# Both products of a gated MLP from seven half products instead of eight, activations stored to DRAM between them

## The chip, the cores and the metric

The kernel runs on one core of one Trainium2 chip. The metric is the device time of one execution in microseconds; the lower, the better. One execution was profiled too: its times are those of the rows below. TensorE is called PE in the rows, VectorE DVE, ScalarE ACT, GpSimd POOL; SP issues most of the DMAs.

## The reference, cut to what matters

A decoder block on 1024 positions of width 1024 in float32: two mixers (sparse attention and retention), merged, an output projection with residual, then an MLP and a final norm. The change lies in the MLP and in what surrounds it:

```python
x = x + (gate_a * y_a + gate_b * y_b) @ w_mix_out[layer]
h = rms_norm(x, norm_ffn_w[layer])
u = causal_dwconv(h @ w_ffn_up[layer], ffn_conv_w[layer], ffn_conv_b[layer])   # 1024 x 5632, width 3
u_gate, u_val = jnp.split(u, 2, axis=-1)
x = x + (jax.nn.silu(u_gate) * u_val) @ w_ffn_down[layer]                      # 2816 x 1024
return rms_norm(x, norm_final_w)
```

## The kernel before

Each float32 product is made in three passes (`mm3`): both operands are split into a high and a low part of the type float32r, and high by high, high by low and low by high are summed in PSUM. A split is one copy on ACT (`wh`, L209, or `ah`, L175) and one subtraction (`wl` on POOL, L215; `al` on DVE, L176). One matmul has 128 rows of contraction, 128 columns of the stationary operand and 512 moving columns.

The output projection (`mo`, from L1044) makes 8 position tiles of 128 in two channel halves. In the second half each tile gets its residual, its RMSNorm and, by `transposed_split`, its place in `h2T`, the transposed and split input of the MLP. Tiles 6 and 7 come out together at the end; their transposes are put between the first up products.

The MLP goes over 11 groups of 256 channels. `up(j)` makes four column tiles (two of the gate, two of the value) over 8 contraction tiles and both halves of the positions, 192 matmuls; `conv` takes each from PSUM: ACT makes the tap of the same position with the bias (L1068), DVE adds the other two (L1069, L1070). Silu, the product with the value (L1095) and the split follow, and the activations stay in SBUF. `down(j-1)` then makes 96 matmuls on the group before, and DVE adds each result to the residual `xr` (L1113). So up and down products take turns, and the weights of a group are loaded by SP and split on ACT and POOL during the group before. The final norm of each tile (`final`, L1116) follows its last down product. A list of instructions is fixed for each engine when the kernel is built; an engine takes them one after the other, each behind the semaphores it waits for.

Of the kernel before, what the change touches and what calls it, by code (L numbers as in the profile page):

```python
# [18 lines left out]
P = 128  # L19
# [144 lines left out]
def hybrid_block(ctx: ExitStack, tc: tile.TileContext, a, c, out):  # L164
# [16 lines left out]
    class Weights:  # L181
        """Rows [k0*128, (k0+nk)*128) by up to 512 columns, split into the two parts of float32r."""
# [46 lines left out]
    def rstd_steps(pool, v):  # L229
        """v ** -0.5, the table's root improved by one step; yields after the root"""  # L230
# [21 lines left out]
    def mean_square(pool, parts, junk):  # L252
        """mean over D of the squares of the parts, plus eps; one part at a time"""
# [15 lines left out]
    def transposed_split(psum, src, hi, lo, t, nk=KT, tag="tp"):  # L269
        """src [128 s, nk*128] -> hi, lo [128, nk, s-tile t]"""  # L270
# [19 lines left out]
    # ---- first norm, transposed and split  # L290
# [7 lines left out]
    big = ctx.enter_context(tc.tile_pool(name="big", bufs=8, side="right"))  # L298
# [77 lines left out]
    def k_store(b, t, ps):  # L376
        """ps [p, (g d)] -> roped, transposed and split keys"""
# [45 lines left out]
    # ---- compressed keys and values  # L423
# [97 lines left out]
    # ---- the three attention branches  # L521
# [5 lines left out]
    def mm3t(ps, w, n0, act, nk, halves=(0, 1)):  # L527
        """ps[n, s] = w columns n0..n0+128 against act(part, kt)"""
# [36 lines left out]
    def scores(box, wait, t, g, bs, rank, last_pe):  # L565
        """Branches bs, the first two in one pass over their keys.
# [625 lines left out]
```

## Time and profile before

| | us |
|---|---|
| median of 3 runs | 1845.14 |
| lowest, highest run | 1844.7, 1846.16 |
| span of the profiled execution, first to last instruction | 1842.4 |
| PE busy in it | 1810.4 (98%) |
| DVE, ACT, POOL busy | 964.9, 694.8, 212.0 |
| up products, start of the first to start of the last matmul | 1105.0 to 1785.2 |
| down products | 1197.3 to 1828.7 |

The profiled execution was not timed apart from its span, so its own time is the span, 1842.4 us; the median of the runs is 2.7 us above that, for what lies ahead of the first and behind the last instruction. A share of busy time is a mean over the span; what bounds a stage is read from that stage.

### The profile page before, as it was taken

The numbers are of one execution on the slowest core, as the hardware profiler recorded it, in microseconds if no ns is written. First come the engines' busy times: TensorE is split into PE (matmuls) and PEld (weight loads), VectorE is DVE, ScalarE is ACT, GpSimd is POOL, SyncE is SP. The second block draws the span as 40 slices with busy tenths as digits, with TensorE's granted clock in tenths as the row PEclk, the third lists the DMA queues.
The fourth block names the chain that finished last, engine by engine and source line by source line (L and its number), as shares of the span: only waits on it lengthen the run. The fifth ranks groups of instructions, "written<-read, shape, count | busy, mean of one in ns | idle before, by whom it ended". The sixth has DMA issues, their size and how long they took to land.

```text
span 1842.4 us, 22342 instructions
## 1 busy us (share of the span) xinstructions
PE 1810.4 (98%) x8727; PEld 1500.7 (81%) x8727; DVE 964.9 (52%) x2062; ACT 694.8 (38%) x1283; POOL 212.0 (12%) x107
## 2 busy tenths in 40 slices
PE   8999999999999999999999999999999999999997
PEld 6987888878788888888888887888888888888885
DVE  7446878777774554564444254344333433424446
ACT  6335676666652352245522133312212211221224
POOL 0000020100000000000000012323113212311204
PEclk9999999999999999999999999999999999999998
DMA  6221020110202111101422411212112102201102
GB/s 223 68 67 52 24 64 24 41 47 24 67 31 81 46 47 46 47 24 46 162 91 79 151 35 30 78 54 69 35 35 69 51 18 69 69 23 46 58 0 103
DMA packets 70230, 110.18 MB, mean 60 GB/s; under 512 B 5532, under 2 KB 37868, under 8 KB 70124
## 3 DMA queue, kind: packets, MB, share of 16 engines
q1 hardware_dynamic: 68828, 104.03, 17.8%
q10 hardware_dynamic: 1296, 4.72, 0.6%
q8 instruction: 68, 1.11, 0.3%
q14 instruction: 38, 0.31, 0.1%
HBM read 96.15 MB, written 12.58 MB: 59 GB/s over the span
## 4 chain that ended last, share of the span: by engine, by line
PE 68%; issue 2%; DVE 2%; ACT 1%; DMA 1%; POOL 0%; SPq 0%; DVEq 0%; ACTq 0%; POOLq 0%
PE up L283 25%; PE mm L283 21%; PE dn L283 12%; PE fill L771 2%; PE mo L283 2%; PE po L825 1%; PE pv L717 1%; PE pt L705 1%; PE sc L609 1%; DMA wr<-in_w_ffn_up 1%; PE pst L825 1%; DVE rs_r L246 1%; PE tp L275 0%; PE pss L870 0%; ACT h L1130 0%
## 5 line engine op out<-in xcount | busy, mean ns | idle before, releaser
L283 PE MATMUL up<-h2T,wh 128*128 128x512 f32 x1408 | 434.0, 389 | 0.2 <-ACT h2T L175 0.2
L215 POOL TENSOR_TENSOR wl<-wr,wh 128x1024 fp32r<-128x1024 f32 x78 | 188.2, 2420 | 1490.4 <-ACT wh L209 1425.8
L283 PEld LDWEIGHTS up<-h2T,wh 128*128 128x128 f32 x1408 | 264.1, 188 | 55.6 <-ACT h2T L175 0.5
L283 PE MATMUL up<-h2T,wl 128*128 128x512 f32 x704 | 274.0, 389 | 0.0
L209 ACT ACTIVATE wh<-wr 128x1024 fp32r<-128x1024 f32 (+1 forms) x138 | 143.2, 1046 | 265.0 <-DMA wr<-in_w_ffn_up 90.2
L1069 DVE SCALAR_TENSOR_TENSOR y<-up,cw,y 128x1023 f32<-128x1023 f32 x44 | 56.4, 1283 | 343.2 <-ACT y L1068 343.2
L283 PE MATMUL mm<-wh,hh 128*128 128x512 f32 (+1 forms) x576 | 224.2, 389 | 0.3 <-ACT hh L175 0.3
L283 PE MATMUL mm<-wh,hl 128*128 128x512 f32 (+1 forms) x576 | 220.0, 382 | 0.0
L283 PE MATMUL mm<-wl,hh 128*128 128x512 f32 (+1 forms) x576 | 219.8, 382 | 0.0
L1068 ACT ACTIVATE y<-up,cw 128x1024 f32<-128x1024 f32 x44 | 53.0, 1204 | 282.7 <-PE up L283 282.5
L283 PEld LDWEIGHTS up<-h2T,wl 128*128 128x128 f32 x704 | 132.2, 188 | 27.5
L1113 DVE TENSOR_TENSOR xr<-dn,xr 128x512 f32<-128x512 f32 x176 | 118.3, 687 | 62.0 <-PE dn L283 62.0
L283 PE MATMUL dn<-wh,ah 128*128 128x512 f32 x352 | 137.1, 390 | 0.1
L283 PE MATMUL dn<-wh,al 128*128 128x512 f32 x352 | 137.0, 389 | 0.0
L283 PE MATMUL dn<-wl,ah 128*128 128x512 f32 x352 | 137.0, 389 | 0.0
L283 PEld LDWEIGHTS mm<-wh,hl 128*128 128x128 f32 x576 | 108.8, 189 | 20.5 <-DVE hl L176 0.3
L283 PEld LDWEIGHTS mm<-wh,hh 128*128 128x128 f32 x576 | 108.9, 189 | 19.9 <-ACT hh L175 0.7
L283 PEld LDWEIGHTS mm<-wl,hh 128*128 128x128 f32 x576 | 108.9, 189 | 19.5 <-DVE wl L215 0.5
L712 DVE TENSOR_TENSOR pl<-pt,ph 128x512 fp32r<-128x512 f32 (+1 forms) x148 | 100.6, 687 | 41.8 <-ACT ph L709 41.2
L709 ACT ACTIVATE ph<-pt 128x512 fp32r<-128x512 f32 (+1 forms) x148 | 87.6, 594 | 82.8 <-PE pt L705 74.5
L771 PE MATMUL fill<-hh,wh 128*128 128x512 f32 x256 | 104.5, 408 | 3.1 <-ACT sg L783 2.1
L627 ACT ACTIVATE big<-big,st 128x640 f32<-128x640 f32 (+7 forms) x128 | 93.4, 730 | 28.1 <-DVE st L623 27.5
(228 smaller groups left out, 3041.6 us busy)
## 6 DMA issues: line engine op xcount, KB each, us to landing
wr<-in_w_ffn_up SPq DMA_DIRECT2D x88, 256.0 KB, 3.2
wr<-in_w_in SPq DMA_DIRECT2D x40, 512.0 KB, 3.7
wr<-in_w_ffn_down SPq DMA_DIRECT2D x22, 512.0 KB, 3.6
gate<-sg SPq DMA_DIRECT2D x32, 256.0 KB, 2.0
wr<-in_w_in SPq DMA_DIRECT2D x16, 256.0 KB, 3.1
wr<-in_w_ret_branch SPq DMA_DIRECT2D x8, 512.0 KB, 4.2
ma<-gate SPq DMA_DIRECT2D x8, 512.0 KB, 6.6
gb<-gate SPq DMA_DIRECT2D x8, 512.0 KB, 7.5
```

The source lines that it names most:

```text
L209: nc.scalar.activation(hi[:, :, :self.n], self.raw[len(self.hi)], AF.Copy)
L215: self.engine.tensor_tensor(lo[:, :, :self.n], self.raw[j], f32(self.hi[j][:, :, :self.n]), OP.subtract)
L246: nc.vector.scalar_tensor_tensor(r, t, -3.0, half, op0=OP.add, op1=OP.mult)
L283: nc.tensor.matmul(ps, stat(sp, kt), mov(mp, kt), start=(first and n == 0), stop=(last and n == 3 * nk - 1))
L627: nc.scalar.activation(probs[b][h], probs[b][h], AF.Exp, scale=-1.0, bias=stat["nm", b][:, h:h + 1], accum_out=stat["w", b][:, h:h + 1])
L709: nc.scalar.activation(bx["h"][:rows], bx["pt"][:rows], AF.Copy)
L712: nc.vector.tensor_tensor(bx["l"][:rows], bx["pt"][:rows], f32(bx["h"][:rows]), OP.subtract)
L771: nc.tensor.matmul(fx["ps"], w.at(sp, kt, i * P, P), hT[mp][:, kt, half * 512:half * 512 + 512], start=(n == 0), stop=(n == 3 * KT - 1))
L825: nc.tensor.matmul(ps[:, h, :], stat[sp][:, h, :], mov[mp][:, h, :], start=(first and n == 0), stop=(last and n == 2))
L1068: nc.scalar.activation(y, ps, AF.Identity, scale=cw[:, 2, f:f + 1], bias=cw[:, 3, f:f + 1])
L1069: nc.vector.scalar_tensor_tensor(y[:, 1:], ps[:, :S - 1], cw[:, 1, f:f + 1], y[:, 1:], op0=OP.mult, op1=OP.add)
L1113: nc.vector.tensor_add(xo, ps, xo)
```

## The change

Everything up to the `mo` products is the same. Behind them both products of the MLP are made by Strassen's scheme in its form of Winograd: positions, contraction and columns are each halved, and seven products of halves of sums are made in place of eight products of halves. The sums are made in float32 ahead of the split.

For up, the columns of the weight are paired by the gate and the value tile of one `f` (22 of them), laid out by the host so that one `f` is one row of 8 KB for each partition (`_up_layout`). The input is cut into quarters by position half and contraction half; three quarters are split as they are (`bh`/`bl` 11, 21, 22), and four sums t1 to t4 are split by `sums(t)`, into memory that is free only when the `mo` products are done. An `f` is seven products of 12 matmuls. What they share is added up on DVE: u2, u3, then cv and cg, the two columns that the convolution reads, now from SBUF. The activations are stored to DRAM (`act_d`), and x1, the residual, too (`x1_d`).

Down starts when up has ended. Its seven products (p1, p2, p5, p6, p3, p7, p4 in that order) run over 11 contraction tiles in six steps of two (`STEPS`) and four position tiles `q`, 132 matmuls each. A step has its operands loaded anew, the weights into a ring of two raw tiles (`wraw`), the activations into tiles that are partly kept (`held`); sums go to POOL (activations) and DVE (weights), and `parts2` splits both. The four position tiles of the first half are normed behind p3, the others behind p4.

```diff
     for ch in range(2):
...
+                if waiting:
+                    piece(*waiting.pop())
+                waiting.append((t, h))
         gw = nx
+    bigs.close()
...
+    for k in ("t1", "t2", "t3", "t4"):
+        bh[k], bl[k] = (tpp.tile([P, 4, 512], F32R, name=f"{part}{k}") for part in ("bh", "bl"))
+
+    def sums(t):
+        at = slice((t - 4) * P, (t - 3) * P)
+        (t1, t4), (t3, t2) = low[t - 4], low[t]
+        for k, x, e in (("t2", t2, nc.gpsimd), ("t3", t3, nc.vector), ("t1", t1, nc.vector), ("t4", t4, nc.gpsimd)):
+            split(bh[k][:, :, at], bl[k][:, :, at], x, e)
+
+    for t in range(4, NT - 1):
+        sums(t)
+    piece(*waiting.pop())
+    sums(NT - 1)
...
+    def parts2(src, engine, cnt=2):
...
+        nc.scalar.activation(hi[:, :cnt], src[:, :cnt], AF.Copy)
+        engine.tensor_tensor(lo[:, :cnt], src[:, :cnt], f32(hi[:, :cnt]), OP.subtract)
+        return hi, lo
...
+    def up(f, w, begun=None):
+        x, p1 = begun or start_up(w)
+        y = bank()
+        prod(y, w["s2"], "t2")
+        u2 = c2()
+        nc.vector.tensor_add(u2, y, p1)
+        q = bank()
+        prod(q, w["s3"], "t3")
+        u3 = c2()
+        nc.vector.tensor_add(u3, q, u2)
+        z = bank()
+        prod(z, w["s1"], "t1")
+        cg, cv = c4(), c4()
+        nc.vector.tensor_add(cv[:, 1], z, u3)
+        if not begun:
+            prod(x, w["a12"], "21", False, True)
+        nc.scalar.activation(cg[:, 0], x, AF.Copy)
+        prod(q, w["a22"], "t4", False, True)
+        nc.vector.tensor_add(cv[:, 0], q, u2)
+        prod(z, w["s4"], "22", False, True)
+        nc.vector.tensor_add(cg[:, 1], z, u2)
+        yg = conv(cg.rearrange("p a b -> p (a b)"), f)
...
+        for n in range(2):
+            nc.sync.dma_start(act_d[f][n], yg[:, n * 512:n * 512 + 512])
...
+    def p5_ops(i, j, n):
+        s, t = store(S2, i), store(T2, i)
+        x, y = held(0, 1, j, n), held(1, 1, j, n)
+        nc.gpsimd.tensor_tensor(s[:, :n], x[:, :n], y[:, :n], OP.add)
+        y, x = raw_w(0, 0, j, n), raw_w(0, 1, j, n)
+        return s, diff(x, y, n, nc.vector, t)
...
+    def p7_ops(i, j, n):
+        s = diff(held(0, 0, j, n), held(0, 1, j, n), n, nc.gpsimd)
+        y, x = raw_w(0, 1, j, n), raw_w(1, 1, j, n)
+        return s, diff(x, y, n, nc.vector, x)
...
+    def down(ps, ops, first, last, tail=0):
+        done = []
+        for i, (j, n) in enumerate(STEPS):
+            s, t = ops(i, j, n)
+            ph, th = parts2(s, nc.gpsimd if i % 2 else nc.vector, n), parts2(t, nc.vector, n)
...
+    down(banks, p3_ops, True, True)
+    for q in range(4):
+        x = x_of(q, 1)
+        add_to(x, banks[q])
+        add_to(x, u[q])
+        add_to(x, p5[q])
+        final(q)
+    banks = [bank() for _ in range(4)]
+    down(banks, p7_ops, True, True)
```

Lines that the diff above leaves out and the rows below name: in the kernel after, L1061 is the transpose of a piece, L1154 to L1160 are the weight sums of an `f`, L1165 the low part of its fourth quarter, L1262 is `diff`, L1282 and L1288 are POOL's sums of p5 and p6, L1329 is `add_to`, L1338 the last step of `final`.

Where `mo` ends, PE's row was this before (`tp` are transposes of tile 6; `h2T_9455` and `h2T_9456` the high and low part of the MLP's input):

```order
4559 L283 MATMUL mo<-wl,mh 128x512
4560 L283 MATMUL mo<-wh,ml 128x512
4561 L275 MATMUL tp<-ident,y 128x128 x8
4562 L283 MATMUL up<-h2T_9455,wh 128x512
4563 L283 MATMUL up<-h2T_9456,wh 128x512
4564 L283 MATMUL up<-h2T_9455,wl 128x512
4565 L283 MATMUL up<-h2T_9455,wh 128x512
4566 L283 MATMUL up<-h2T_9456,wh 128x512
```

The 8 transposes of tile 6 stand first and those of tile 7 24 matmuls later. Now the row at the same place is this (`bh_9441` and `bl_9444` are the two parts of quarter 11; every bank is called `f`):

```order
4559 L283 MATMUL f<-wl,mh 128x512
4560 L283 MATMUL f<-wh,ml 128x512
4561 L1061 MATMUL f<-ident,h 128x128 x24
4562 L283 MATMUL f<-bh_9441,wh 128x512
4563 L283 MATMUL f<-bl_9444,wh 128x512
4564 L283 MATMUL f<-bh_9441,wl 128x512
4565 L283 MATMUL f<-bh_9441,wh 128x512
4566 L283 MATMUL f<-bl_9444,wh 128x512
4567 L283 MATMUL f<-bh_9441,wl 128x512
4568 L283 MATMUL f<-bh_9441,wh 128x512
```

All 24 transposes of tiles 5, 6 and 7 now stand ahead of the first up matmul.

POOL's row before is 78 times the same instruction, `wl<-wr,wh` of L215, in the MLP and ahead of it. Now, from the end of p2 into p5, it is this (`st` are the sums kept for p5 and p6, `c_14345` and its like the sums of p3):

```order
80 L1288 TENSOR_TENSOR st<-st,act 128x1024
81 L1262 TENSOR_TENSOR c_14345<-c_14345,st 128x1024
82 L1282 TENSOR_TENSOR st<-act 128x1024
83 L1139 TENSOR_TENSOR wl<-st,wh 128x1024
84 L1288 TENSOR_TENSOR st<-st,act 128x1024
85 L1262 TENSOR_TENSOR c_14383<-c_14383,st 128x1024
86 L1282 TENSOR_TENSOR st<-act 128x1024
87 L1288 TENSOR_TENSOR st<-st,act 128x1024
88 L1262 TENSOR_TENSOR c_14421<-c_14421,st 128x1024
89 L1282 TENSOR_TENSOR st<-act 128x1024
90 L1139 TENSOR_TENSOR wl<-st,wh 128x1024
91 L1288 TENSOR_TENSOR st<-st,act 128x1024
```

Between the sum of one step of p5 (L1282) and that of the next stand the sum of p6 (L1288) and that of p3 (L1262) for the step before.

Before, DVE had only the additions of L1113 and the steps of `conv` between the splits of the MLP. Now, where p3 ends and p7 begins, its row is this (`c_13843`, `c_14560`, `c_13846`, `c_14585` are the halves of tiles 0 and 1 of the result):

```order
2027 L1338 SCALAR_TENSOR_TENSOR c_13843<-c_13843,rs_r,c_13411 128x512
2028 L1338 SCALAR_TENSOR_TENSOR c_14560<-c_14560,rs_r,c_13411 128x512
2029 L246 SCALAR_TENSOR_TENSOR rs_r<-rs_t,rs_h 128x1
2030 L1338 SCALAR_TENSOR_TENSOR c_13846<-c_13846,rs_r,c_13411 128x512
2031 L1338 SCALAR_TENSOR_TENSOR c_14585<-c_14585,rs_r,c_13411 128x512
2032 L1139 TENSOR_TENSOR wl<-c_14664,wh 128x1024
2033 L1139 TENSOR_TENSOR wl<-wr,wh 128x1024
2034 L1329 TENSOR_TENSOR c_14610<-f,c_14610 128x512
2035 L1329 TENSOR_TENSOR c_14610<-c_13630,c_14610 128x512
```

The two splits (L1139) of p7's first step have moved behind the norm of the first two result tiles.

## Rows read from the trace of the kernel before

**Rows 1.** The page: busy time by engine, and TensorE's granted clock in 40 slices
```profile
PE 1810.4 (98%) x8727; PEld 1500.7 (81%) x8727; DVE 964.9 (52%) x2062; ACT 694.8 (38%) x1283; POOL 212.0 (12%) x107
PEclk9999999999999999999999999999999999999998
```

**Rows 2.** The chain that ended last: start us, length us, engine, tile, line
```profile
1742.04 43.53 PE up L283 x192
1785.57 29.94 PE dn L283 x132
```

**Rows 3.** Windows of the MLP and of its end: busy us by engine, granted clock
```profile
core 0: us, PE busy (x) PEld busy (x) DVE busy (x) ACT busy (x) POOL busy (x), PEclk, DMA share, GB/s
1105.00:1114.00 9.00, 6.76 (x36) 5.44 (x35) 5.54 (x11) 5.52 (x11) 4.76 (x2) 1.00 0.41 126
1197.00:1785.00 588.00, 587.92 (x2593) 486.33 (x2593) 227.87 (x252) 132.60 (x123) 122.97 (x51) 1.00 0.15 47
1831.00:1833.00 2.00, 0.00 (x0) 0.00 (x0) 2.00 (x4) 1.06 (x2) 1.09 (x2) 0.97 0.49 187
1833.00:1835.00 2.00, 0.00 (x0) 0.00 (x0) 1.64 (x5) 1.60 (x6) 2.00 (x2) 0.50 0.26 97
```

**Rows 4.** Tiles mo, up and dn: last kind of matmul, ns min/median/max, first and last start
```profile
L283 PE MATMUL mo<-wh,ml x128: 390/393/404, 1010.9 to 1104.0; 128*128 128x512 f32 x128
...
L283 PE MATMUL up<-h2T,wl x704: 388/389/400, 1105.6 to 1785.2; 128*128 128x512 f32 x176
...
L283 PE MATMUL dn<-wh,al x352: 388/389/396, 1197.7 to 1828.7; 128*128 128x512 f32 x176
```

**Rows 5.** Groups by line and shape, 1105 to 1829 us: busy us, mean ns of one
```profile
L215 POOL TENSOR_TENSOR wl<-wr,wh 128x1024 fp32r<-128x1024 f32 x63 | 151.8, 2417 | 544.5 <-ACT wh L209 480.0 <-PE dn L283 60.3 <-PE up L283 4.2
L1113 DVE TENSOR_TENSOR xr<-dn,xr 128x512 f32<-128x512 f32 x174 | 117.0, 687 | 62.0 <-PE dn L283 62.0
L209 ACT ACTIVATE wh<-wr 128x1024 fp32r<-128x1024 f32 x63 | 65.5, 1056 | 103.3 <-DMA wr<-in_w_ffn_up 88.5 <-PE up L283 14.8
L1069 DVE SCALAR_TENSOR_TENSOR y<-up,cw,y 128x1023 f32<-128x1023 f32 x44 | 56.4, 1283 | 343.2 <-ACT y L1068 343.2
L1068 ACT ACTIVATE y<-up,cw 128x1024 f32<-128x1024 f32 x44 | 53.0, 1204 | 282.7 <-PE up L283 282.5
L176 DVE TENSOR_TENSOR al<-y,ah 128x1024 fp32r<-128x1024 f32 x22 | 27.0, 1226 | 14.1 <-ACT ah L175 14.1
L1095 DVE TENSOR_TENSOR y<-y 128x1024 f32<-128x1024 f32 x22 | 26.9, 1221 | 0.4
```

**Rows 6.** DMA issues of the page: KB of each, median us from issue to landing
```profile
wr<-in_w_ffn_down SPq DMA_DIRECT2D x22, 512.0 KB, 3.6
```

**Rows 7.** Timeline of TensorE at the start: start us, length us
```profile
8.51 1.97 PE L275 MATMUL tp<-ident,big 128*128 128x128 f32 x8 [8.51 <-DVE big L267]
13.13 0.63 PE L283 MATMUL mm<-wl,hh 128*128 128x512 f32 x1
13.56 0.63 PE L283 MATMUL mm<-wh,hl 128*128 128x512 f32 x1
```

**Rows 8.** Timeline of a final norm: start us, length us
```profile
1833.28 0.62 ACT L256 ACTIVATE h<-xr 128x512 f32<-128x512 f32 x1
1833.40 0.16 DVE L236 RECIPROCAL rs_y<-rs_s 128x1 f32<-128x1 f32 x1 [0.30 <-ACT rs_s L233]
1834.13 1.12 DVE L246 SCALAR_TENSOR_TENSOR rs_r<-rs_t,rs_h 128x1 f32<-128x1 f32 x1
1835.34 0.75 DVE L1133 SCALAR_TENSOR_TENSOR h<-xr,rs_r,gain 128x512 f32<-128x512 f32 x1
```

**Rows 9.** Timeline of DVE and POOL in a down group: start us, length us
```profile
1269.94 1.23 DVE L176 TENSOR_TENSOR al<-y,ah 128x1024 fp32r<-128x1024 f32 x1
1270.93 2.52 POOL L215 TENSOR_TENSOR wl<-wr,wh 128x1024 fp32r<-128x1024 f32 x1 [5.75 <-ACT wh L209]
...
1278.53 2.40 POOL L215 TENSOR_TENSOR wl<-wr,wh 128x1024 fp32r<-128x1024 f32 x1 [2.72 <-ACT wh L209]
```

More of the change, by code (lines that the diff above doesn't have):

```diff
@@ L276, in transposed_split, with mm3 @@
             split(hi[:, k:k + n, t * P:(t + 1) * P], lo[:, k:k + n, t * P:(t + 1) * P], ps[:, :n, :])
-    def mm3(ps, stat, mov, nk, first=True, last=True):
+    def mm3(ps, stat, mov, nk, first=True, last=True, more=False):
         n = 0
@@ L1166, in hybrid_block @@
-    with tc.manual_schedule(engines={PE, DVE, ACT, POOL}):
-        last_down(dw)
+                h = [mx.tile([P, 512], F32, name="h", bufs=3) for _ in range(2)]
+                *_, v = mean_square(mx, x1[t], h)
+                r = rstd_of(mx, v)
+                for n in range(2):
+                    nc.vector.scalar_tensor_tensor(h[n], x1[t][n], r, gain2[:, n * 512:n * 512 + 512], op0=OP.mult,
+                                                   op1=OP.mult)
+                    nc.sync.dma_start(x1_d[t][n], x1[t][n])
@@ new lines, in hybrid_block @@
+    uw = {}
+    begun = {}
+    LEAD = 2
+    for f in range(LEAD):
+        uw[f] = up_weights(f)
+        begun[f] = start_up(uw[f])
+    for f in range(LEAD):
+        prod(begun[f][0], uw[f]["a12"], "21", False, True)
+    for f in range(FT):
+        if f + 1 < FT and f + 1 not in uw:
+            uw[f + 1] = up_weights(f + 1)
+        up(f, uw.pop(f), begun.pop(f, None))
+    tp.close()
+    ups.close()
+    HT = FT // 2
+    STEPS = [(j, min(2, HT - j)) for j in range(0, HT, 2)]
+    rp_ = ctx.enter_context(tc.tile_pool(name="act", bufs=16, side="right", reuse_waits="tile"))
@@ new lines, in hybrid_block, with x_of, add_to @@
+    xs = {}
+    def x_of(t, n):
+        if (t, n) not in xs:
+            xs[t, n] = c2()
+            nc.sync.dma_start(xs[t, n], x1_d[t][n])
+        return xs[t, n]
+    def add_to(dst, src, engine=None):
+        (engine or nc.vector).tensor_tensor(dst, src, dst, OP.add)
+    def final(t):
+        x = [xs.pop((t, n)) for n in range(2)]
+        junk = c4()
+        *_, v = mean_square(small, x, [junk[:, n] for n in range(2)])
+        r = rstd_of(small, v)
+        for n in range(2):
+            c = slice(n * 512, n * 512 + 512)
+            nc.vector.scalar_tensor_tensor(x[n], x[n], r, gain3[:, c], op0=OP.mult, op1=OP.mult)
+            nc.sync.dma_start(out[0, t * P:(t + 1) * P, c], x[n])
@@ new lines, in hybrid_block @@
+    banks = [bank() for _ in range(4)]
+    down(banks, p1_ops, True, True)
+    u = []
+    for q in range(4):
+        u.append(c2())
+        nc.scalar.activation(u[q], banks[q], AF.Copy)
+    down(banks, p2_ops, False, True)
+    for q in range(4):
+        add_to(x_of(q, 0), banks[q])
+    banks = [bank() for _ in range(4)]
+    down(banks, p5_ops, True, True)
+    p5 = []
+    for q in range(4):
+        p5.append(c2())
+        nc.scalar.activation(p5[q], banks[q], AF.Copy)
+    banks = [bank() for _ in range(4)]
@@ L1170, with _up_layout @@
+    banks = [bank() for _ in range(4)]
+    down(banks, p4_ops, True, True, tail=2)
+    for q in range(4):
+        add_to(x_of(4 + q, 0), banks[q])
+        final(4 + q)
+def _up_layout(w):
+    w = w[0].reshape(2, KT // 2, P, 2, FT, P)
+    return np.ascontiguousarray(w.transpose(4, 2, 3, 0, 1, 5)).reshape(FT, P, 4 * 512)
+_LAYOUT = {"w_ffn_up": _up_layout}
 _OUT = ((1, S, D), "float32")
```

291 lines of the change are left out of this document (172 added, 119 removed).

## The prediction

> **What bounds the kernel now.** I read the page's busy lines first: TensorE is busy 98% of the span, in nearly every slice, at the full granted clock [rows 1]. The chain that ended last says the same of the MLP: from 1120 us to the end it is up and down products in turn, 192 matmuls in 43.53 us, 132 in 29.94 us [rows 2], that is 0.2267 us for each 128x512 matmul. The last output-projection matmul starts at 1104.0 and so ends at 1104.2, the last down matmul starts at 1828.7 and ends at 1828.9 [rows 4]. Between them lie 2112 up and 1056 down matmuls, 3168 x 0.2267 = 718.2 us of work in 724.7 us: TensorE loses only 6.5 us in the whole MLP, most of it beside the last transposes (in 1105 to 1114 it is busy 6.76 of 9 us) [rows 3]. Behind the last matmul 13.5 us of final norm and stores remain (1842.4 - 1828.9). So before the change every matmul taken away is time taken away, and DVE (228 us of 588), ACT and POOL have room [rows 3]. The question is whether they still have it afterwards.
>
> **What is removed.** Seven half products for eight: up 22 x 84 = 1848 for 2112, down 7 x 132 = 924 for 1056. 396 fewer matmuls of 128x512, at 0.2267: **-89.8 us**. The 6.5 us that before loses go too and are charged anew below. The length of matmuls does not change, so I take their pace from before.
>
> **Mix stage.** The matmuls up to the last output product are the same. The first transposes of channel half 1 wait longer for their norm; x1 and its store are off the path. +0.8 us, so the last output matmul ends at E = 1105.0.
>
> **From the output projection to up (+23.1).** Before, half of the positions are transposed in time, and up matmuls on them fill the wait for tiles 6 and 7. Now the first up product stands behind all 24 transposes of tiles 5, 6 and 7. Tiles 6 and 7 come out of the last pair together, and each needs add 0.69, Square 0.62 and its accumulator read, root, small DVE steps of up to 1.1, two multiplications of 0.75 [rows 5, 8]; on DVE tile 7's follow tile 6's, with Strassen sums between. By hand: tile 6 transposed at E+6, tile 7 at E+12.3. Product one (12 matmuls, 2.7 us) ends at E+15.0. The next 12 accumulate into its bank, so they wait for the copy of it (p1), which on ACT stands behind the splits of t1 to t4 of tile 7; and these wait for four sums in turn on DVE and POOL (0.69 and half of 2.42 each) [rows 5]: E+20.3. Then f=1: its raw weights go into a ring of two, whose slots are released by L1159 (DVE, E+19.8) and L1165 (POOL, E+22.4), both queued behind the same sums. Load (512 KB as down's: 3.6 us) [rows 6], ACT 1.06, POOL 2.42 [rows 5]: E+29.7. By then TensorE has done 29 matmuls, 6.6 us. Lost: 23.1; bounds 19 (if the sums run at the back-to-back pace) and 27.
>
> **Up in its steady state (0).** An f lasts 84 x 0.2267 = 19.05 us. DVE needs in it five 128x512 sums from PSUM (0.69), four convolution steps (1.28), one product (1.22), four 512-wide weight sums and two splits (1.23) [rows 5]: 15.0 us. ACT has some 8.5, POOL 3.7. But it is a ring: the last product of f ends, and cg1, a weight sum, four convolution steps, sum, product, sum, split, sum, u2 and u3 must be through on DVE, with one ACT Identity of 1.2 ahead, before product a22 of the next f can overwrite u3's bank, 13.6 us later. Added up: 12.55 us. TensorE stays the bound with 1 us to spare; the DMA of 1 MB per f is small.
>
> **From up to down (+7.1).** Let U be the end of up. The first down weight's low part (L1139) is on DVE behind cg1, a split and the four convolution steps of f=21: 0.7 + 1.2 + 1.06 of ACT + 4 x 1.2 = U+8.0. Four matmuls (0.9) run before it.
>
> **Down.** Each product has five steps of 24 matmuls (5.44 us) and a half one; unstalled it lasts 29.9 us. Products one and two load 512 KB of weights and as much of activations in a step, split on ACT, DVE and POOL: within 5.44.
> - *p5 (+16.3).* POOL makes its sums, and its instructions are in a row: between p5's sum of step 1 and that of step 2 it makes p6's and p3's (L1288, L1262) too. In two steps it has six additions and a split of 2.42 [rows 5] and waits once for ACT (1.2) and once for ACT and DVE (2.4): 20.5 us, against 10.9 of TensorE. Its row starts about 5.7 us ahead of p5. So step 2 can go at +18.4 from p5's start, step 4 at +39.0, and the end is at +46.2. The weight side is not the later one: two loads and the difference, 6 us a step.
> - *p6 and p3 (+3).* Their sums are there; each start waits 1 to 2 us for a difference and split.
> - *p3 to p7 (+11.0).* The split of p7's first weight sum (second of two L1139) is on DVE behind the final norms of tiles 0 and 1: six additions from 2.0 us before the end of p3, a table load (1.3) and the root on ACT, small steps, four multiplications, two splits. It ends 11.9 us after p3; four matmuls run before.
> - *p7's steps (+10.6).* Both raw slots go into one difference made in place, so the next load waits for the split: 3.6 and issue 0.4, 1.23, 1.06, 1.23 [rows 5, 6] and the signals between, 7.9 us a step against 5.44; stores of `out`, and loads of x1 waiting for room, stand in SP's row ahead of the weights and keep it from getting ahead.
> - *p7 to p4 (+8.6).* p4's first difference stands on DVE behind twelve additions (7.4 us), and a difference and a split more.
>
> **The clock (+4).** Behind the last matmul of before the granted clock falls from 1.00 to 0.50 about four us on [rows 3], 2.4 to 1.2 GHz. At the start, after 8.5 us without matmuls, they come 0.43 us apart instead of 0.23, for some ten of them [rows 7]: 2 us. After the change TensorE is without a matmul for over four us at six places; at four the step behind them waits for data anyway. Two count.
>
> **Tail (-1.7).** Final norms of four tiles start together, two Squares each, then one multiplication and store each: 11.8 for 13.5 us.
>
> **Sum.** -89.8 - 6.5 + 0.8 + 23.1 + 7.1 + 16.3 + 3 + 11.0 + 10.6 + 8.6 + 4 - 1.7 = -13.5 us. The profiled span is 1842.4, the median of the runs 1845.1: 2.7 us lie around the span, and I leave them. 1842.4 - 13.5 = 1828.9, so **1832 us**. Of 90 us that are saved, 76 are given back at places where TensorE finds nothing prepared.
>
> **The rivals.**
> *Feeds keep up (B).* My p5 and p7 sums rest on the order of rows and on loads of 3.6 us. If POOL gets well ahead in p1 and p2, or the loads come in pairs sooner, p5, p6 and p7 run at TensorE's pace, and 16.3 + 2 + 10.6 go: 1803 us. For it: POOL was busy 123 of 588 us [rows 3] and DMA moves little; against it: rows on one engine cannot pass each other.
> *DVE's ring in up (C).* The same side as no gain: the place is u3 ahead of a22, the slack is 1 us. If the chain of 12.55 takes 15% more (signals between 13 instructions; in before DVE has gaps of 0.05 to 0.1 there), each f takes 0.8 us more, 22 of them 18 us: 1850 us, slower than before. It decides from 0.6 us per f beyond the slack. For it: DVE was busy 39% of the stretch and is now at 79%; against it: back to back, its instructions come sooner than their length.
> *POOL and DVE in each other's way (D).* The one split of POOL that began beside a DVE instruction with two SBUF inputs took 2.52 us, and 2.40 without it: 0.12 for 0.24 us of overlap, half [rows 9]. In p5 some 15 us of such DVE work falls into POOL's full row: +7 us by that; with POOL standing still, +15. The Trainium skill (GPSIMD Engine Reference, 8. Key points) has a rule that speaks against this change: POOL shares its SBUF interfaces with VectorE and contends with DVE instructions that have two SBUF inputs. By that rule the time comes out at 1839 to 1847; the trace agrees in direction, with 0.12 us.
>
> **How the numbers follow.** A change under 0.2%, 3.7 us, is about what a measurement of this kernel cannot tell from none: 1841.4 to 1848.8. As costed (A): 0.42, own range 1815 to 1848 (each bound above by a third), so 0.34 faster, 0.05 same, 0.03 slower. B: 0.27, all faster. C: 0.15, of it 0.13 slower. D, or the clock falling at more places (six times 2 us, +8): 0.16, as 0.06, 0.06 and 0.04. Faster 0.67, same 0.13, slower 0.20. The range takes in most of B and C: 1796 to 1858.
>
> **What would show it.** In the profile after: 1848 and 924 matmuls still 0.2267 us apart inside a product (else the first term fails); TensorE's idle time released by ACT and POOL from E to E+30; no idle time of TensorE between two f's (if there is, and DVE full, C); p5 of 46 us with POOL full, p7 of 40 us with SP's weight loads after DVE's splits (if 30 each, B); 9 to 12 us without matmuls between p3, p7 and p4, a clock row of 0.5 there. I would be wrong by most if up's f is not 19.05 us, since that counts 22 times.

## The result, and the profile after

The changed kernel takes 1870.4 us (median of 4 runs, 1868.6 to 1874.8) against 1845.6 us of the kernel before in the same job: ratio 1.0139, 95% interval 1.0125 to 1.0153. It is slower by 1.4%, where 0.7% faster was forecast, and outside the range. The profiled execution has a span of 1873.1 us; the sum of the prediction came to 1828.9 for it, so 44 us are to be found. It is the longest of the four, 4.4 us above their median; where these 4.4 lie is not shown.

The page of the changed kernel, busy time and granted clock in 40 slices, answers to [rows 1]:

```profile
PE 1765.1 (94%) x8331; PEld 1442.8 (77%) x8331; DVE 1175.7 (63%) x2266; ACT 801.7 (43%) x1464; POOL 253.0 (14%) x133
PEclk9999999999999999999999988999999998979888
```

TensorE has 396 instructions fewer, worth 89.8 us, and is busy only 45.3 us less: its matmuls have become slower, some at half the clock behind a wait, some in up for a reason of their own (below). The span holds 108 us in which it does nothing, against 32 before. DVE and POOL are busy 211 and 41 us more.

The chain that ended last, with start, length and count, answers to [rows 2]: from 1150 us on up is one piece of TensorE's work, with no wait in it, though 416.08 us for so many is more than 0.2267 each.

```profile
1150.29 416.08 PE f L283 x1802
...
1814.82 7.21 DVE c L1329 x12
...
1828.94 4.11 DMA wr<-in_w_ffn_down
...
1834.38 3.35 DVE wl L1139
1837.74 3.34 DMA wr<-in_w_ffn_down
...
1843.56 2.65 DMA wr<-in_w_ffn_down
```

In p7 and p4 it is another one: twelve additions of DVE when p7 has ended, and then p4's loads of raw weights, each behind a split.

Windows answer to [rows 3]: busy us of each engine, its instructions, the granted clock. They are the start of up in two rows, up, five us behind a wait of p1, and p5.

```profile
core 0: us, PE busy (x) PEld busy (x) DVE busy (x) ACT busy (x) POOL busy (x), PEclk, DMA share, GB/s
1106.00:1123.00 17.00, 5.11 (x25) 3.67 (x24) 15.76 (x24) 11.67 (x26) 10.31 (x7) 0.67 0.08 31
1123.00:1150.00 27.00, 16.33 (x49) 11.79 (x47) 23.27 (x21) 10.55 (x15) 15.92 (x10) 0.77 0.17 56
1170.00:1560.00 390.00, 390.00 (x1693) 317.26 (x1692) 284.66 (x325) 165.74 (x180) 69.38 (x38) 1.00 0.26 83
...
1577.00:1582.00 5.00, 5.00 (x13) 3.83 (x13) 5.00 (x3) 0.00 (x0) 1.77 (x1) 0.50 0.58 201
...
1638.50:1691.80 53.30, 39.08 (x133) 28.63 (x132) 30.13 (x21) 13.47 (x15) 41.84 (x16) 0.81 0.33 109
```

Where TensorE waits, its own timeline says: in brackets the idle time before a matmul, and who ended it. The first two rows stand between up and down, the third in p5, the others at the start of p7 and of p4.

```profile
1570.55 2.08 PE L283 MATMUL f<-wh 128*128 128x512 f32 x4 [4.18 <-ACT wh L1138]
1576.61 0.79 PE L283 MATMUL f<-wl,wh 128*128 128x512 f32 x1 [3.99 <-DVE wl L1139]
...
1681.80 2.07 PE L283 MATMUL f<-wh 128*128 128x512 f32 x4 [6.83 <-ACT wh L1138]
...
1763.59 2.07 PE L283 MATMUL f<-wh 128*128 128x512 f32 x4 [7.32 <-ACT wh L1138]
1770.48 0.79 PE L283 MATMUL f<-wl,wh 128*128 128x512 f32 x1 [4.82 <-DVE wl L1139]
...
1824.39 1.22 PE L283 MATMUL f<-wh 128*128 128x512 f32 x2 [8.28 <-ACT wh L1138]
```

These waits stand where the prediction put them. The surprise is in the rows of the engines that they wait for. DVE and POOL in p5, and in the last rows of each between p3 and p7, which answer to [rows 9]:

```profile
1640.51 2.10 DVE L1139 TENSOR_TENSOR wl<-st,wh 128x1024 fp32r<-128x1024 f32 x1
...
1655.21 1.23 DVE L1139 TENSOR_TENSOR wl<-st,wh 128x1024 fp32r<-128x1024 f32 x1 [5.72 <-ACT wh L1138]
...
1760.56 2.39 DVE L239 SCALAR_TENSOR_TENSOR rs_t<-rs_y,rs_v 128x1 f32<-128x1 f32 x1
...
1762.93 0.20 DVE L239 SCALAR_TENSOR_TENSOR rs_t<-rs_y,rs_v 128x1 f32<-128x1 f32 x1
```

```profile
1645.15 3.27 POOL L1288 TENSOR_TENSOR st<-st,act 128x1024 f32<-128x1024 f32 x1
1648.49 3.25 POOL L1262 TENSOR_TENSOR c<-c,st 128x1024 f32<-128x1024 f32 x1
1651.70 2.38 POOL L1282 TENSOR_TENSOR st<-act 128x1024 f32<-128x1024 f32 x1
...
1758.28 4.65 POOL L1262 TENSOR_TENSOR c<-act 128x1024 f32<-128x1024 f32 x2 [12.33 <-ACT c L256]
```

The same shape takes POOL 3.25 or 2.38, and DVE 2.10 or 1.23, as the other engine works beside it or not. The last two rows of DVE are a small step on one number for each partition, 0.20 us; beside the second of the two sums in POOL's last row it took 2.39.

The boundaries of the stages, against the prediction's sum (us; a product ends with the start of its last matmul and 0.23):

| stage | predicted | measured | difference |
|---|---|---|---|
| end of the output projection | 1105.0 | 1106.2 | +1.2 |
| from it to the end of up, 1566.2 | 442.1 | 460.0 | +17.9 |
| up to p2's end, 1638.5 | 67.0 | 72.3 | +5.3 |
| p5, to 1691.8 | 46.2 | 53.3 | +7.1 |
| p6 and p3, to 1756.1 | 62.9 | 64.3 | +1.4 |
| p7, to 1815.9 | 51.5 | 59.8 | +8.3 |
| p4, to 1861.5 | 38.5 | 45.5 | +7.0 |
| behind it | 11.8 | 11.6 | -0.2 |
| the clock, costed apart | 4 | in the rows above | -4 |

The +1.2 of the first row means nothing: in the other kernels with the same start, run below, this point lies between 1103.4 and 1107.7.

### The profile page after: what moved, and what is told of

The parts are those of the page before. It is cut to its first block, busy times and chain, and to the rows that moved or that the text cites. A ratio compares the mean times of both kernels' runs of the same rounds, so it can differ in the third digit from the quotient of the medians.

```text
span 1873.1 us, 22357 instructions
## 1 busy us (share of the span) xinstructions
PE 1765.1 (94%) x8331; PEld 1442.8 (77%) x8331; DVE 1175.7 (63%) x2266; ACT 801.7 (43%) x1464; POOL 253.0 (14%) x133
## 4 chain that ended last, share of the span: by engine, by line
PE 62%; DVE 6%; POOL 2%; DMA 2%; issue 1%; ACT 1%; DVEq 0%; SPq 0%; ACTq 0%; POOLq 0%
PE f L283 33%; PE mm L283 21%; PE fill L772 2%; DVE wl L1139 1%; DMA wr<-in_w_ffn_down 1%; PE po L826 1%; PE pv L718 1%; DVE c L1329 1%; PE pt L706 1%; ACT wh L1138 1%; PE sc L610 1%; DVE c L1338 1%; POOL c L1262 1%; POOL st L1282 1%; PE pst L826 1%
## 5 line engine op out<-in xcount | busy, mean ns | idle before, releaser
L1139 POOL TENSOR_TENSOR wl<-wr,wh 128x1024 fp32r<-128x1024 f32 x22 | 52.8, 2401 | 901.4 <-ACT wh L1138 901.4
L283 PE MATMUL f<-wh 128*128 128x512 f32 x308 | 123.6, 424 | 38.0 <-ACT wh L1138 38.0
L283 PE MATMUL f<-wl,wh 128*128 128x512 f32 x308 | 130.1, 422 | 18.4 <-DVE wl L1139 18.0
L283 PE MATMUL f<-wh,wl 128*128 128x512 f32 x308 | 126.8, 412 | 0.0
L283 PE MATMUL f<-bh,wh 128*128 128x512 f32 x264 | 105.3, 399 | 11.0 <-ACT c L1184 7.9
L215 DVE TENSOR_TENSOR wl<-wr,wh 128x1024 fp32r<-128x1024 f32 (+1 forms) x60 | 71.5, 1192 | 57.9 <-ACT wh L209 57.0
L1138 ACT ACTIVATE wh<-wr 128x1024 fp32r<-128x1024 f32 (+1 forms) x52 | 52.9, 1017 | 125.6 <-PE f L283 68.1
L283 PEld LDWEIGHTS f<-wh 128*128 128x128 f32 x308 | 61.7, 204 | 56.2 <-ACT wh L1138 43.2
L283 PE MATMUL f<-bht,wl 128*128 128x512 f32 x264 | 104.5, 396 | 0.0
L283 PE MATMUL f<-bl,wh 128*128 128x512 f32 x264 | 104.5, 396 | 0.0
L283 PE MATMUL f<-bht,wh 128*128 128x512 f32 x264 | 104.4, 396 | 0.0
```

Of the source, the lines that this page charges most:

```text
L215: self.engine.tensor_tensor(lo[:, :, :self.n], self.raw[j], f32(self.hi[j][:, :, :self.n]), OP.subtract)
L1138: nc.scalar.activation(hi[:, :cnt], src[:, :cnt], AF.Copy)
L1139: engine.tensor_tensor(lo[:, :cnt], src[:, :cnt], f32(hi[:, :cnt]), OP.subtract)
```

## The experiments

Two theories stood against each other. **Turns**: POOL and DVE do not both work on SBUF when DVE's instruction reads two operands there, so each holds up the other, and my durations, from rows of one engine alone, were too short. **Order**: the durations hold, and the order of rows, the loads and the clock cost more than I summed. Below, kernels are compared by their medians; the median of the kernel before moved between 1843.6 and 1845.6 us from one set of runs to the next, so a difference under 3 us says nothing by itself.

**One engine beside the other.** A kernel that does nothing of the block: stages of 8 additions of 128x1024 on POOL beside 16 instructions on DVE.

```diff
+        for k in range(8):
+            if stage != 4:
+                nc.gpsimd.tensor_tensor(po, xb[:, 1], xb[:, 2], OP.add)
+            if stage == 1 or stage == 4:
+                for _ in range(2):
+                    nc.vector.tensor_tensor(do, xb[:, 3], xb[:, 4], OP.add)
+            elif stage == 2:
+                for _ in range(2):
+                    nc.vector.tensor_tensor(do, ps, xb[:, 4], OP.add)
+            elif stage == 3:
+                for _ in range(2):
+                    nc.vector.tensor_scalar(do, xb[:, 3], 2.0, None, OP.mult)
```

> Nothing of the reference is computed: five stages of additions of 128x1024 in SBUF, to time the two engines by themselves. Stage 0: 8 on POOL alone; stage 1: 8 on POOL beside 16 on DVE with two inputs in SBUF; stage 2: the same with one DVE input in PSUM; stage 3: DVE multiplies one SBUF tensor by a number; stage 4: 16 on DVE alone. Theory S (the engines share a way into SBUF, and a DVE instruction with two SBUF inputs takes turns with POOL): POOL 2.40 us in stages 0, 2 and 3 and about 3.3 in stage 1; DVE 1.23 in stages 2 and 4 and 2 to 3 in stage 1 while POOL runs. Rival O (each engine keeps its length; what was late in the changed kernel is order, clock and DMA): 2.40 and 1.23 in every stage.

Timelines of POOL and of DVE (start, length of all x, operation):

```profile
13.72 19.25 POOL L185 TENSOR_TENSOR po<-xb 128x1024 f32<-128x1024 f32 x8 [13.28 <-DMA xb<-in_x]
...
34.14 26.33 POOL L185 TENSOR_TENSOR po<-xb 128x1024 f32<-128x1024 f32 x8
...
71.37 19.32 POOL L185 TENSOR_TENSOR po<-xb 128x1024 f32<-128x1024 f32 x8
...
92.44 22.06 POOL L185 TENSOR_TENSOR po<-xb 128x1024 f32<-128x1024 f32 x8
```

```profile
34.09 36.27 DVE L188 TENSOR_TENSOR do<-xb 128x1024 f32<-128x1024 f32 x16 [0.40 <-POOL po L182]
...
71.33 20.10 DVE L191 TENSOR_TENSOR do<-ps,xb 128x1024 f32<-128x1024 f32 x16 [0.40 <-POOL po L182]
...
92.39 27.75 DVE L194 TENSOR_SCALAR do<-xb 128x1024 f32<-128x1024 f32 x16 [0.40 <-POOL po L182]
...
121.30 20.12 DVE L188 TENSOR_TENSOR do<-xb 128x1024 f32<-128x1024 f32 x16 [0.40 <-POOL po L182]
```

Alone, POOL needs 2.41 us for one (19.25 / 8) and DVE 1.26 (20.12 / 16). Side by side with two SBUF operands POOL needs 3.29 (26.33 / 8). Of DVE's 36.27 us, 9.89 are left when POOL has ended, enough for 8 at 1.26; so the other 8 ran in POOL's 26.33, one for each of POOL's, 3.29 each. With one operand in PSUM both keep their pace (2.41, 1.26). That is the turns theory, with its price: a pair takes 3.29 where 3.67 would be one behind the other and 2.41 both at once. In one stage the theory missed: beside a multiplication of one SBUF tensor by a number POOL takes 2.76 (22.06 / 8), not 2.40.

**The mix stage's sums on DVE.** The changed kernel with the sums and splits of `sums(t)` and `piece` on DVE.

```diff
-        nc.gpsimd.tensor_tensor(b12, b22, b12, OP.subtract)
+        nc.vector.tensor_tensor(b12, b22, b12, OP.subtract)
...
-        nc.gpsimd.tensor_tensor(b21, b21, b22, OP.subtract)
+        nc.vector.tensor_tensor(b21, b21, b22, OP.subtract)
...
-        for k, x, e in (("t2", t2, nc.gpsimd), ("t3", t3, nc.vector), ("t1", t1, nc.vector), ("t4", t4, nc.gpsimd)):
+        for k, x, e in (("t2", t2, nc.vector), ("t3", t3, nc.vector), ("t1", t1, nc.vector), ("t4", t4, nc.vector)):
```

> The sums and low parts that POOL makes of the MLP's input (L1074, L1076, t2 and t4 of L113's split) go to DVE; the rest is as changed. From the end of the output products to the first full up product, 44.1 us now. Theory S: POOL's turns go, DVE's instructions of 1.7 us are 0.7 again; 32 to 36 us, 1858 to 1862 us in all. Rival O: DVE has 4 x 0.65 us more for each of three tiles on the chain that everything waits for; 48 to 52 us, 1874 to 1878 in all.

1867.0 us, ratio 1.0126 [1.0111, 1.0141]: 3.4 less than the changed kernel, which the spread of the runs hardly tells from none (1865.4 to 1871.2 here, 1868.6 to 1874.8 there), and a miss of both theories' times. The start of up is as the turns theory had it, 32 to 36 us, and the trace tells the gain better than the medians. The chain:

```profile
1133.28 0.61 DVE c L1159
...
1133.95 3.63 DMA wr<-in_w_ffn_up
...
1137.61 1.06 ACT wh L1138
...
1138.74 2.38 POOL wl L1139
...
1141.16 421.71 PE f L283 x1820
```

Up is in full course 33.5 us after the output projection's end (1107.7 here), 44.1 in the changed kernel, 29.7 predicted. The chain is the predicted one (L1159 releases a slot, load 3.6, copy, split on POOL). From the projection's end to up's end it is 455.0 us for 460.0, so 5.0 of the 10.6 are kept: up goes on for 421.5 us from there, for 415.9, since fewer of its matmuls were made before. Between up and down 2.1 are lost again, since a split on DVE falls beside POOL there: full down comes 12.5 us after up's end, 10.4 in the changed kernel.

**Up alone from seven.** Down as 1056 matmuls, streamed in two halves of the positions (weights read twice).

```diff
+    for half in range(2):
+        banks = [[bank() for _ in range(2)] for _ in range(4)]
...
+        for kt in range(FT):
...
+            for q in range(4):
+                for n in range(2):
+                    mm3(banks[q][n], lambda part, _: ap2[part][:, q * P:(q + 1) * P],
+                        lambda part, _: wp2[part][:, n, :], 1, kt == 0, kt == FT - 1)
```

> Strassen in up alone; down is plain, 1056 matmuls, 24 for each of 22 activation tiles read back from DRAM, in two halves of the positions, split on ACT, DVE and POOL. It parts the loss between the halves of the change. As the trace after has it (up ends at 1566, down would need 6 + 239.4 + 1 us and a tail of 13): 1826 to 1832 us, so that up gains some 15 us net and Strassen's down costs 40 against a plain one. If up with its start were what loses: over 1845.

1823.4 us, ratio 0.9883 [0.9866, 0.9899], a little under the 1826 to 1832. Seven products pay in up. In down they cost 47 us (1870.4 - 1823.4), though they have 132 matmuls, 29.9 us, less.

**Down's sums on DVE.** The changed kernel with the sums and splits that POOL makes in down on DVE, six lines like these:

```diff
-        nc.gpsimd.tensor_tensor(s[:, :n], x[:, :n], y[:, :n], OP.add)
+        nc.vector.tensor_tensor(s[:, :n], x[:, :n], y[:, :n], OP.add)
...
-            ph, th = parts2(s, nc.gpsimd if i % 2 else nc.vector, n), parts2(t, nc.vector, n)
+            ph, th = parts2(s, nc.vector, n), parts2(t, nc.vector, n)
```

> Every sum and split of Strassen's down on DVE, none on POOL. Theory S: in p5 DVE has 6 instructions of 1.23 us for a step, 7.4 us, with no turns of POOL's; p5 41 to 44 us instead of 53.5, p7 3 to 6 us shorter; 1853 to 1860 us. Rival O: DVE takes over some 11 us of work in p7 and as much in p5, on the engine that the starts of p7 and p4 wait for; 1875 to 1882 us.

1844.5 us, ratio 0.9999 [0.9990, 1.0008]: 26 us less than the changed kernel, more than either theory's number. In p5 DVE's timeline reads:

```profile
1639.72 1.22 DVE L1262 TENSOR_TENSOR st<-wr 128x1024 f32<-128x1024 f32 x1
...
1641.99 1.22 DVE L1288 TENSOR_TENSOR st<-st,act 128x1024 f32<-128x1024 f32 x1
```

Three more sums on DVE and it is through sooner: one of POOL's and one of DVE's together take 3.3 us, both on DVE 2.3 (starts 1.13 apart). From up's end to p5's end it is 106.1 us; the changed kernel has 125.6, my sum, with POOL at 2.42 undisturbed, 113.2. So of the 19 us some 12 are what my sum had missed, turns and slow matmuls among it, and 7 that POOL alone is slower; this split is argued from my sum, not measured.

**The ring of raw weights.** The kernel above, and p7's and p4's raw weights in the pool of the held differences (`st`) in place of the ring of two.

```diff
-    def raw_w(kh, nh, j, n):
-        r = wraw.tile([P, 2, 512], F32, name="wr")
+    def raw_w(kh, nh, j, n, pool=None):
+        r = (pool or wraw).tile([P, 2, 512], F32, name="st" if pool else "wr")
...
-        y, x = raw_w(0, 1, j, n), raw_w(1, 1, j, n)
+        y, x = raw_w(0, 1, j, n, stp), raw_w(1, 1, j, n, stp)
...
-        r = raw_w(1, 0, j, n)
+        r = raw_w(1, 0, j, n, stp)
```

> The kernel is the one with all sums of down on DVE (1844.5 us), and p7's and p4's raw weights take their room from the pool of the held differences, where it is free, in place of the ring of two. In that kernel p7's 132 matmuls last 46.7 us from their first (1743.1 to 1789.7) and p4's 33.4. If the ring of raw loads sets p7's steps, as my sum had it (load 3.6, difference 1.23, copy 1.06, split 1.23, signals, 7.9 us a step), p7 comes to 30 to 35 us and p4 to 30 to 31, and the time to 1828 to 1833. If DVE's own row sets them (final norms, additions and splits), p7 stays within 3 us of 46.7 and the time at 1842 to 1846.

1832.6 us, ratio 0.9937 [0.9921, 0.9954], 12 less. From p3's end to p7's end it is 43.2 us (1737.1 to 1780.3) for 54.7, and from p7's first matmul 34.9, as the ring's theory had it; p4, from there to its end 38.9, is not the 30 to 31 expected. From p3 on TensorE's timeline has only the starts of p7 and p4 left as long waits:

```profile
1745.37 2.07 PE L283 MATMUL f<-wh 128*128 128x512 f32 x4 [8.11 <-ACT wh L1138]
...
1787.14 0.80 PE L283 MATMUL f<-wl,wh 128*128 128x512 f32 x1 [5.82 <-DVE wl L1139]
```

**The same edit alone**, on the changed kernel, POOL's sums left where they are.

> The changed kernel with one edit: p7's and p4's raw weights in the free pool; POOL keeps its sums in down. On top of the sums on DVE this edit was worth 12 us. If it is a cause of its own, 10 to 14 us come back: 1856 to 1860. If POOL's and DVE's turns set p7's steps as well, so that the ring alone does little, under 5 us: 1865 to 1870.

1854.0 us, ratio 1.0058 [1.0041, 1.0074], 16.4 less than the changed kernel, so the ring is a cause of its own. The chain where p4 begins:

```profile
1803.52 1.22 DVE wl L1139
...
1813.55 25.99 PE f L283 x104
```

With 104 of p4's 132 matmuls from 1813.55 on, the other 28 stand before it, and p4 begins at 1804.75, when the split of its first step is done. So p7 is 50.9 us (1753.8 to 1804.7) for 59.8, and p4 34.6 (to 1839.4) for 45.5 (20 us together, but the changed kernel's profiled execution lies 4.4 above its median). With room for p4's loads its differences are made during p7, and most of the twelve additions run beside the matmuls of its first step; TensorE waits there for 2.3 us, where the changed kernel has 8.3. p7, with POOL beside DVE in it, is still 7.7 us longer than where DVE makes the sums and the ring is gone too (43.2).

**No norm between p3 and p7.** The changed kernel; tiles 0 to 3 are stored as they are before the final norm.

```diff
-        final(q)
+        for n in range(2):
+            nc.sync.dma_start(out[0, q * P:(q + 1) * P, n * 512:n * 512 + 512], xs.pop((q, n)))
```

> The changed kernel without the final norm of tiles 0 to 3: those tiles are stored as they are before the norm. The work on DVE between p3 and p7 loses four multiplications and small steps, ACT loses eight Squares and the roots; POOL keeps its sums. In the changed kernel p7's first matmul comes 7.3 us after p3's last and its full pace 14.2 us after. If the norms ahead of the split in DVE's row set this, as my prediction had it, full pace comes 4 to 8 us after p3 and p7 itself is shorter by a few us more, in all 8 to 14 us: 1856 to 1862. If what sets it is the weights' load into the ring, or DVE's twelve-addition row alone, less than 4 us comes back: 1866 to 1871.

1858.7 us, 11.7 less than the changed kernel (ratio to before 1.0077 [1.0062, 1.0092]). TensorE's timeline around p3's end, 1756.9:

```profile
1757.24 0.50 PE L283 MATMUL f<-wh 128*128 128x512 f32 x1 [0.20 <-ACT wh L1138]
1758.50 0.50 PE L283 MATMUL f<-wl,wh 128*128 128x512 f32 x1 [0.76 <-DVE wl L1139]
...
1769.52 2.08 PE L283 MATMUL f<-wh 128*128 128x512 f32 x4 [5.51 <-ACT wh L1138]
```

p7's first step follows p3 at once, and the second waits 5.5 us for the additions. p3's end to p7's end is 46.2 us for 59.8. DVE's order changes with the edit, so this shows that the norms in DVE's row cost this much there, not that their work alone does.

**Up alone, with the sums on DVE,** and **with two products ahead.** First the edit of the second experiment on up alone from seven. Then, in addition, the first `f`'s two products that need only what is transposed by then (24 matmuls) between the transposes of tile 5 and those of tiles 6 and 7:

```diff
+                if t == NT - 1:
+                    early(0)
                 if waiting:
                     piece(*waiting.pop())
```

> Up from seven products and down streamed as eight, in two halves of the positions (1823.4 us), with the sums and splits of the mix stage on DVE in place of POOL. In the changed kernel the same edit brought full up 7 to 9 us sooner but only 3.4 us of the time, the rest was given back in down. If the loss was down's own, the whole 7 to 9 us is kept here: 1814 to 1818. If the edit itself brings no more than 3.4 us, because up's ring runs behind all the same: 1819 to 1821.

> The kernel of e7, and the two products of the first f that need only the positions transposed by then (24 half products, 5.4 us) are put between the transposes of tile 5 and those of tiles 6 and 7, in banks of their own; their sum is then made on DVE. If TensorE's wait ahead of up is for tiles 6 and 7, as the prediction had it, the 5.4 us of work fill it and the time is 4 to 6 us under e7's. If up starts no sooner because f=1's weights and the sums of the last tiles on DVE end last anyway, the gain is under 2 us.

1818.8 us, ratio 0.9861 [0.9846, 0.9875], and 1814.9, ratio 0.9841 [0.9826, 0.9855]: 4.6 and 3.9 less. Neither theory of the first named 4.6; the end of up comes 456.2 us after the projection's end, 460.0 without the edit, so it is what the start of up kept. The second is a little under its theory's 4 to 6. TensorE's timeline there still shows a wait of 13.9 us for the sums and weights of the rest of the first `f`:

```profile
1133.67 0.79 PE L283 MATMUL f<-bht,wh 128*128 128x512 f32 x1 [13.86 <-ACT wh L1082]
```

**All mends together,** both products from seven.

> Both products from seven half products, with all mends together: the sums and splits of the mix stage and of down on DVE, p7's and p4's raw weights in the free pool, and the first two up products between the transposes. The mends lie in stages that follow each other. If each keeps its worth: 1832.6 less 4.6 less 3.9, that is 1822 to 1826, faster than before, but 7 to 11 us slower than up alone from seven (1814.9). If what is won ahead of up is given back in down: 1828 to 1833.

1823.1 us, ratio 0.9885 [0.9871, 0.9900]: the gains add up. It is 1.2% faster than before and still 8 us slower than up alone from seven with the same mends (1814.9).

**Where the operands begin.** In the changed kernel an `f` of up lasts 19.37 us (DVE's last sum of it, L1205, starts at 1408.68 and seven groups on at 1544.29), not 19.05, though TensorE never waits. Row by row, matmuls on t1 to t4 come 0.2335 apart, those on the quarters 0.2267. A kernel with rows of 48 matmuls alone, on operands cut from one tile at chosen places:

```diff
+    places = [("lo", 65536, 352), ("lo", 65536, 2016), ("hi", 180224, 352), ("hi", 180224, 2016), ("lo", 65536, 0),
+              ("hi", 180224, 0), ("mid", 122880, 352), ("mid", 122880, 2016)]
...
+    for n, m in enumerate(mv):
+        run(1 + n % 4, st_lo, m)
+    run(5, st_hi, mv[0])
+    run(6, st_hi, mv[3])
+    run(7, st_lo, mv[0])
```

> A kernel that does nothing of the block: 48 matmuls of 128x512 in a row for each of ten pairs of places in SBUF, with no other engine at work, after 60 to begin with. In the changed kernel an up group lasts 19.37 us where 84 x 0.2267 is 19.05: matmuls whose moving operand is one of the sums t1 to t4 come 0.2335 us apart, those on the plain quarters 0.2267. The sums lie at 160 KB and above in each partition and begin 32 bytes ahead of a multiple of 2 KB, the quarters lie at 50 to 100 KB and begin 352 bytes behind one. If the begin counts, the three rows of 48 that begin 32 bytes ahead last 11.2 us and all others 10.9, wherever they lie. If the height counts, the three at 176 KB and above last 11.2 and those below 10.9. If neither does, because what counts is the other engines' work on the same memory, all ten last 10.9.

The chain (start, length), in the order of the edit, without four rows that say the same again. The third number of a place is the begin of the moving operand, in bytes behind a multiple of 2 KB. The stationary operand is one of four slices in turn, 512 bytes apart, the first of which begins 352 bytes behind such a multiple, in `bf` and `bg` 2016 behind one:

```profile
26.70 10.88 PE bb L196 x48
37.58 11.19 PE bc L196 x48
48.77 10.89 PE bd L196 x48
59.66 11.19 PE be L196 x48
...
82.09 11.24 PE bc L196 x48
...
115.43 11.20 PE bf L196 x48
126.63 10.90 PE bg L196 x48
```

I had expected that the begin counts for itself. It is neither that nor the height: `be` and `bg` have the same moving operand at 2016, and take 11.19 with the stationary one at 352 and 10.90 with one at 2016. In these rows a matmul is quick when both operands begin at the same place of a block. That block is at most 512 bytes, since the slices of a quick row are 512 apart, and more than 128, since 352 and 2016 are the same place of 128. By the addresses in the built program, the changed kernel's weights begin at 352 and t1 to t4 at 2016.

**The same begin.** The kernel with two products ahead (1814.9 us), with 128 bytes left free, so that t1 to t4 begin where the weights do within 512 bytes:

```diff
+    pad = tp.enter_context(tc.tile_pool(name="pad", bufs=1, side="right"))
+    pad.tile([P, 32], F32, name="pad")
     tpp = tp.enter_context(tc.tile_pool(name="tp", bufs=1, side="right", reuse_waits="tile"))
```

> The kernel of e8, and 128 bytes of each partition left free above t1 to t4, so that they begin 352 bytes behind a multiple of 512, as the weights do. By the rows of 48 before this, a matmul is slow when its two operands begin at different places of a block (11.2 us for 48) and quick when they begin at the same (10.9), whatever the place is. If a block is 512 bytes or less, an up group comes to 19.05 us for 19.37 and the time to 22 x 0.32 = 7 us less, 1806 to 1810. If a block is 1 or 2 KB, or if other engines' work on these tiles is what costs, the group stays at 19.37 and the time at 1813 to 1817.

1806.4 us, ratio 0.9799 [0.9783, 0.9816]: 8.5 less, the fastest of all that ran. From the projection's end to up's end it is 444.7 us for 451.8, the 7 us expected; the other 1.6 lie ahead of the projection's end, which this edit does not touch. An `f` is 19.05 us (1393.96 to 1413.01 for that sum). The chain's piece of up, first without the 128 bytes:

```profile
1145.02 406.88 PE f L283 x1763
```

```profile
1143.39 399.93 PE f L283 x1763
```

So the begins are the cause in the kernel too, and other engines' work on these tiles is not.

## Why the prediction was wrong

**What held.** The waits are the predicted ones, and in sum as long: all terms but the clock's sum to 104 us without work for TensorE in the whole span (32, less 6.5, plus the losses costed), and 108 were measured. TensorE never waits in up's steady state (390.00 busy of 390), so rival C, DVE's ring, fell; rival B, that the feeds keep up, fell too. The tail came to 11.6 for 11.8. What grew is TensorE's own time: 44.5 us more than the 1720.6 (1810.4 - 89.8) that the full pace leaves. Some of it lies on the path and some fills waits: in p5 TensorE is busy 39.1 of 53.3 us for matmuls worth 29.9. That the waits come to the predicted sum is luck in part: by the list below the feeds took longer than costed, and the slower matmuls filled what that added. What set each stage is told by the runs.

**The first step that failed** is the sentence "The length of matmuls does not change, so I take their pace from before". In up 48 of 84 matmuls took 0.2335, 22 x 0.32 = 7 us. The sign stood in the rows: `mo` has a median of 393 ns, `up` and `dn` 389 [rows 4]; by the addresses in the built program, the two operands of `mo` begin 352 and 480 bytes behind a multiple of 512 in the kernel before, those of `up` both at 352, those of `dn` both at 480. I read these rows for their starts alone. In down, too, matmuls are slower: behind each long wait they come 0.43 us apart for a while, at a granted clock of 0.50, 1.2 GHz (13 from 1576.6 us on, 0.2 each, are half of the 5.3 us that p1 and p2 lost). The +4 for the clock is too small for that; but in p5 and p7, where the feeds end last, a slow matmul fills a wait, and edits of the feeds alone took 17 us off p5 and 17 off p7.

**The second** is the cost of one instruction, "2.42" for POOL and "1.23" for DVE [rows 5], used wherever both work. Those rows come from a kernel in which the two seldom meet, and in the one meeting that I read [rows 9] DVE had begun first: it shows POOL's loss, 0.12 us, and cannot show DVE's, which is the larger (1.26 to 3.29 where POOL never pauses). Rival D had the mechanism, but with 7 to 15 us, in p5 alone, and with a part of 0.16 of the chance. It sits in every term with POOL in it:

- *From the output projection to up, costed 23.1.* To the end of up it is 17.9 longer; 7 of it are the begins, 10.9 the start. With the sums on DVE the start in earnest is at 33.5 behind the projection, 3.8 behind the predicted 29.7, for 44.1, and 5.0 of it are kept at up's end. What is left, 5.9, no run takes apart; the granted clock is 0.67 and 0.77 in that stretch.
- *p5, costed +16.3.* POOL is the one that p5 waits for, as costed, but at 3.25. Step 4 begins 43.3 us behind p5's begin (1681.80), for the costed 39.0. Of the +7.1 these 4.3 come from POOL's row, in which six sums up to there took 3.2 to 3.4; 1.9 are slow matmuls behind that wait (10.0 us for 8.2), and 1.0 is a slip of the sum: 39.0 and a step and a half end at 47.2, not 46.2. So rival D's +7 is met here by its mechanism in part, and in part by luck.
- *p3 to p7 and p7's steps, costed +11.0 and +10.6.* Both mechanisms are shown: without the norms p7's first step waits no more, and with room for the raw weights p7 is 8.9 us shorter, 11.5 with the sums on DVE, near the +10.6 of the term. Of the 8.3 us that p7 lost beyond, 5.1 go with the sums on DVE.
- *p7 to p4, costed +8.6.* The twelve additions stand there word for word, but the sum stopped at p4's start. p4's raw weights go through the same ring, with a difference made in place, and I had charged that to p7 alone. This is a term left out, not one mis-sized. Its loads (4.11, 3.34, 2.65) stand in the chain of the changed kernel above, each behind a split, and with room for them p4 is 10.9 us shorter.

**What spoke against the change.** A sum on POOL beside one on DVE with two SBUF operands takes 3.29 us for the pair, a size that the trace before had hidden. The Trainium skill (GPSIMD Engine Reference, 8. Key points) says that POOL shares its SBUF interfaces with VectorE and contends with DVE instructions in a two-port mode or with two SBUF inputs. The runs agree. The same list says that for elementwise work DVE is about twice as fast; 2.41 against 1.26 agrees. Rival D, with this mechanism, ends at 1847, 23 us short; it was charged in p5 alone.

**Size of the causes,** each by a run without it: POOL's part in down 26 us, POOL's part ahead of up 3 to 5, the ring of raw weights 12 to 16, the begins of t1 to t4 7. Taken away they give more than the 44 us, since they also shorten waits that the sum had costed rightly. With the first three gone the seven products in down still cost 264.5 us from up's end to the end (1558.2 to 1822.7), the eight 255.3 (1561.6 to 1816.9): 29.9 us of matmuls are saved and 39 lost. Of these, 26 are time without a matmul, most of it at the seams (8.1 at p7, 6.0 at p4, 4.2 and 1.9 at the start), and 13 are slower matmuls (TensorE busy 223.9 us for 209.5 worth of them, with eight products 241.1 for 239.4). Up has no such seams, since its 22 groups are alike and each is prepared during the one before.

## What to carry to other kernels

Before work is given to POOL because it is idle, look at what DVE does in the same stretch: with two SBUF operands on DVE the pair is slower than DVE doing both, and DVE loses too, which a row that POOL joined late does not show. Here fewer matmuls paid where one group's operands are made during the group before, and not where each product starts anew behind loads, sums and norms; and a ring charged to one product is to be charged to every product that goes through it. When a matmul's operand moves to another tile, compare its pace in rows of both places, by hundredths of a microsecond: it counts as often as the matmul does.

## What was unexpected of the hardware

A matmul of 128x512 takes 0.227 us when its two operands begin at the same place within 512 bytes of a partition, and 0.233 at the pairs of other places that were tried, at all heights in SBUF that were tried (10.9 and 11.2 us for 48). DVE's multiplication by a number, with one SBUF operand, also meets POOL: of 16 in 27.75 us, 8 run beside POOL's 8, which take 22.06 us, 2.76 for a pair, and the rest is 0.7 for one. With one of a DVE sum's two operands in PSUM nothing is lost on either side. And an instruction of DVE on 128x1 lasted through one of POOL's sums, 2.39 us for 0.20.
